# Differential attention: each query block split once and placed by transfers two heads ahead, norms over two heads at a time

## The chip, the cores and the metric

The program runs on one core of one Trainium2 chip. The metric is device time in microseconds (us) of one execution, the median over several executions. The core has a matrix engine (TensorE, PE in the rows, with its weight loads shown as PEld), three engines for elementwise work (VectorE or DVE, ScalarE or ACT, GpSimd or POOL), and a queue engine, SyncE or SP, that issues transfers. Each engine works through its own list of instructions in order and waits on semaphores of the others.

## The reference

Two layers of a hybrid block run over 512 latent tokens and a prefix of 256 context tokens, width 1024. What matters here is head group B, differential attention: 4 heads, each with two query/key halves of 64 columns (m = 0, 1) and one value of 128 columns. Behind it the output of a head is normed and joined with the other groups by an output projection:

```python
def diff_attn(q, k, v, lam):
    s = jnp.einsum("bqhmd,bkhmd->bhmqk", q, k) * (B_QK_DIM ** -0.5)
    p = jax.nn.softmax(s, axis=-1)
    a = p[:, :, 0] - lam * p[:, :, 1]
    return jnp.einsum("bhqk,bkhd->bqhd", a, v)
...
    yb = rms_norm(o, P["subln_g"]) * (1.0 - lam_init)
...
    return jnp.concatenate([ya, yb, yc], axis=-1) @ P["w_out"]
```

Latent queries see 512 latent and 256 context keys in one softmax; context queries see the 256 context keys, and only in the first layer are their outputs needed.

## The kernel before

Large products are made in a split form: a number is written as a high part that TensorE takes at its faster rate (fp32r) and the rest as a second fp32r number, so that a product is two or three matmuls. `sub_lo(o, a, hi)` (line 119) makes the rest, a subtraction on VectorE; a cast makes the high part. `act(...)` (line 110) is a ScalarE function, `flip` (line 122) a transpose on TensorE.

The attention stage of a layer (lines 845 to 1000) goes over a list of what the code numbers by `n`: a head and a block of 256 queries. In layer 0 these are 4 heads of context (2 key tiles of 128, so 256 keys) and then 8 of latent (4 heads, two blocks of 256 queries each, 6 key tiles, 768 keys); in layer 1 only the 8 of latent. The text calls each of them a head, context or latent. A head has two halves of 128 queries, `units (n, i)`. For a unit the loop calls `scores` and `combine`; two units later `transp` turns the weights around, three units later `attn_v` multiplies them with the values once for both halves, and five units later `subln` norms the head's output:

- `q_prep(n)`: TensorE transposes the queries into `pq`; ScalarE casts them once to `qn`; then the high part has to lie in both halves of the partitions, once for each m, and ScalarE and GpSimd copy it there, two 64x256 casts each (line 882). The rest goes to one of two tiles `qlz`, half of which was filled with zeros once per layer (lines 849 to 855), by two `sub_lo` of 64x256. Head 0 is cast straight from `pq` by four ScalarE casts (line 872).
- `scores(n, i)`: for each m two matmuls per stretch of keys (high, line 899, and rest, line 900), the row maximum on VectorE (`mx`, line 902) and the exponential with its sum on ScalarE (`e`).
- `combine(n, i)`: on VectorE `cc` (lines 915 and 916) and `e0 += cc*e1` (line 918); on GpSimd `dg`, a diagonal tile with epsilon times the squared sum (line 919): the weights are not divided by their sum, so the norm's epsilon is scaled instead.
- `transp(n, i)`: transposes into `pat`; the copies into `ath` are ScalarE's for the first four key tiles (line 935) and VectorE's for the last two (line 937).
- `attn_v(n)`: `po`, the copy `o`, its square `osq` (both ScalarE), and `osq + dg` on GpSimd (line 952).
- `subln(n)`: a product with ones (`pr`, line 959), logarithm and exponential (ScalarE), `o*gsub*osq` (VectorE, line 962), and the two parts `yBh` (ScalarE, line 964) and `yBl` (VectorE, line 119).

In the loop head n+1's queries are made when head n's first unit begins. Between these, TensorE takes parts of the output projection that don't need group B, `wo` in the rows, as filler; their weights are loaded through SP (`raw<-in_w_out_dram`), split into `whi` (ScalarE) and `wlo` (VectorE or GpSimd), and their sums added into `xT` (line 835). The order on each engine is decided when the program is built, by a list scheduler with priorities: the loop gives the emission order, `tc.high_priority(offset=SCP)` moves q_prep and scores ahead, and fillers go where the scheduler thinks that TensorE is free.

## Time and profile before

| | us |
|---|---|
| three runs | 1578.26, 1577.02, 1573.16 |
| their median | 1577.02 |
| the profiled execution | 1576.31 |
| its span, first to last instruction | 1574.5 |

The profile is of one execution; 1.8 us of its time lie around the span. Positions are us from the start of the span. The attention stage of layer 0 goes from about 237 to 345, that of layer 1 from about 1101 to 1186. Rows give, for a group of instructions, the count, the busy time, the mean duration of one, and the idle time of the engine just before with what ended it. A matmul's listed duration has a modelled tail that the next one overlaps, so a TensorE that shows as busy can be less than full.

### The profile page before, as it was taken

Reading aid. Unit: us, or ns where it says so; the run is one execution under the profiler, and the core shown is the slowest. Engines: PE = TensorE matmul, PEld = TensorE weight load, DVE = VectorE, ACT = ScalarE, POOL = GpSimd, SP = SyncE. Lnnn points to the kernel's source line nnn. Section 1 sums busy time; section 2 is a strip of 40 time slices with the busy share of each in tenths; the row PEclk is TensorE's granted clock in tenths of the full one; section 3 lists DMA queues with packets and bytes.
Section 4 is the critical chain, followed back from the end, with each engine's and each line's share of the span. In section 5 each row is a group of like instructions: output and inputs, shape, how many; then the busy total and the mean of one; then the engine's idle time right before and its main releaser. Section 6 shows DMA issues by size and latency. Waiting matters only on the chain.

```text
span 1574.5 us, 22904 instructions
## 1 busy us (share of the span) xinstructions
PE 1537.3 (98%) x8804; PEld 1305.1 (83%) x8804; DVE 1128.5 (72%) x1916; ACT 693.3 (44%) x1212; POOL 125.0 (8%) x144
## 2 busy tenths in 40 slices
PE   6999998999999999999999999999999999999999
PEld 4767776778788888888888887887778798998897
DVE  4489878969999982555555556796996974785673
ACT  5423578752532221123334234245774663463461
POOL 1102125310000000000000000000421200000000
PEclk9999999999999999999999999999999999999999
DMA  7651110015265885666877867653002353453432
GB/s 284 236 200 64 54 54 14 14 42 200 69 195 185 281 266 181 239 211 212 287 255 249 286 228 250 202 174 107 28 16 79 124 171 108 166 187 116 154 115 94
DMA packets 89486, 251.89 MB, mean 160 GB/s; under 512 B 12960, under 2 KB 15264, under 8 KB 89248
## 3 DMA queue, kind: packets, MB, share of 16 engines
q1 hardware_dynamic: 89376, 250.43, 47.6%
q8 instruction: 69, 1.13, 0.3%
q14 instruction: 41, 0.34, 0.1%
HBM read 211.59 MB, written 38.80 MB: 159 GB/s over the span
## 4 chain that ended last, share of the span: by engine, by line
PE 74%; DVE 3%; ACT 1%; issue 0%; POOL 0%; DVEq 0%; ACTq 0%; POOLq 0%
PE pp L359 9%; PE pp L358 9%; PE pp L360 9%; PE pd L358 7%; PE pd L360 7%; PE pd L359 7%; PE sv L358 4%; PE sv L359 4%; PE sv L360 4%; PE acc L528 2%; PE acc L536 2%; PE acc L529 2%; PE wo L358 2%; PE wo L359 2%; PE wo L360 2%; PE po L947 1%
## 5 line engine op out<-in xcount | busy, mean ns | idle before, releaser
L119 DVE TENSOR_TENSOR wlo<-raw,whi 128x1024 fp32r<-128x1024 f32 (+2 forms) x176 | 209.8, 1195 | 165.5 <-ACT whi L271 139.7
L271 ACT CAST whi<-raw 128x1024 fp32r<-128x1024 f32 (+1 forms) x137 | 139.5, 1021 | 402.3 <-PE pd L359 152.7
L359 PE MATMUL pp<-hlo,whi 128*128 128x256 f32 (+1 forms) x784 | 267.0, 342 | 1.5 <-DVE hlo L401 1.1
L358 PE MATMUL pp<-hhi,whi 128*128 128x256 f32 (+1 forms) x784 | 266.1, 341 | 1.3 <-ACT whi L271 1.0
L360 PE MATMUL pp<-hhi,wlo 128*128 128x256 f32 (+1 forms) x784 | 265.0, 339 | 0.0
L358 PE MATMUL pd<-gh,whi 128*128 128x512 f32 (+1 forms) x540 | 191.2, 354 | 0.0
L359 PE MATMUL pd<-gl,whi 128*128 128x512 f32 (+1 forms) x540 | 190.6, 353 | 0.0
L360 PE MATMUL pd<-gh,wlo 128*128 128x512 f32 (+1 forms) x540 | 190.6, 353 | 0.0
L359 PEld LDWEIGHTS pp<-hlo,whi 128*128 128x128 f32 x784 | 147.4, 188 | 22.8 <-DVE hlo L401 4.8
L358 PEld LDWEIGHTS pp<-hhi,whi 128*128 128x128 f32 x784 | 147.3, 188 | 22.0 <-ACT whi L271 2.5
L360 PEld LDWEIGHTS pp<-hhi,wlo 128*128 128x128 f32 x784 | 147.4, 188 | 18.2 <-DVE wlo L119 0.2
L360 PEld LDWEIGHTS pd<-gh,wlo 128*128 128x128 f32 x540 | 101.5, 188 | 15.6
L359 PEld LDWEIGHTS pd<-gl,whi 128*128 128x128 f32 x540 | 101.6, 188 | 15.2
L358 PEld LDWEIGHTS pd<-gh,whi 128*128 128x128 f32 x540 | 101.5, 188 | 15.1
L778 DVE SCALAR_TENSOR_TENSOR cacc<-cin,cw,cacc 128x783 f32<-128x783 f32 (+1 forms) x120 | 104.9, 925 | 3.4 <-ACT cacc L773 3.4
L243 DVE CUSTOM_DVE_ANT_0 mraw<-mraw,csil,bmod 128x1024 f32<-128x1024 f32 x64 | 81.6, 1278 | 5.9 <-DMA mraw<-in_w_modT_dram 5.7
L359 PE MATMUL sv<-hlo,whi 128*128 128x256 f32 x288 | 81.2, 282 | 0.0
L358 PE MATMUL sv<-hhi,whi 128*128 128x256 f32 x288 | 81.1, 282 | 0.0
L360 PE MATMUL sv<-hhi,wlo 128*128 128x256 f32 x288 | 81.1, 282 | 0.0
L1174 ACT CAST whi<-raw 128x1024 fp32r<-128x1024 f32 x54 | 56.5, 1050 | 51.2 <-PE sv L359 32.8
L528 PE MATMUL acc<-whi,hhi 128*128 128x512 f32 x192 | 78.6, 409 | 0.0
L529 PE MATMUL acc<-whi,hlo 128*128 128x512 f32 x192 | 76.5, 399 | 0.0
(279 smaller groups left out, 3335.2 us busy)
## 6 DMA issues: line engine op xcount, KB each, us to landing
raw<-in_w_gv_dram SPq DMA_DIRECT2D x78, 512.0 KB, 4.1
mraw<-in_w_modT_dram SPq DMA_DIRECT2D x64, 512.0 KB, 4.3
raw<-in_w_down_dram SPq DMA_DIRECT2D x37, 512.0 KB, 3.9
pgv<-in_w_gv_dram SPq DMA_DIRECT2D x28, 512.0 KB, 5.5
gv<-pgv SPq DMA_DIRECT2D x28, 512.0 KB, 4.7
raw<-gv SPq DMA_DIRECT2D x28, 512.0 KB, 3.8
wh<-in SPq DMA_DIRECT2D x24, 512.0 KB, 4.5
wl<-in SPq DMA_DIRECT2D x24, 512.0 KB, 4.6
```

The source lines that it names most:

```text
L119: return (eng or V).tensor_sub(o, a, hi.bitcast(F32))
L243: r = V.tensor_tensor_reduce(out=junk, in0=w, in1=csil[:, s], scale=1.0, scalar=bmod[:, l, i, f:f + 1], op0=ALU.mult, op1=ALU.add, accum_o ...
L271: S.copy(hi, raw)
L358: T.matmul(o, lhi, rhi, start=start, stop=False, skip_group_check=again)
L359: T.matmul(o, lhi, rlo, start=False, stop=False, skip_group_check=again)
L360: T.matmul(o, llo, rhi, start=False, stop=stop, skip_group_check=again)
L528: T.matmul(pt[t], hhi[hs], wh[:, a], start=k2 + a == 0, stop=False)
L529: T.matmul(pt[t], hlo[hs], wh[:, a], start=False, stop=False)
L536: T.matmul(pt[t], hhi[hs], wl[:, a], start=False, stop=k2 + 1 == KD // 2 and a == 1)
L778: V.scalar_tensor_tensor(out=cacc[:, c, :cn], in0=cin[:, c, j:j + cn], scalar=cw[:, l, c, j:j + 1], in1=cacc[:, c, :cn], op0=ALU.mult, op1 ...
L947: T.matmul(po, vt[:, kt, hs], at[:, c], start=c == 0, stop=c == nk - 1)
L1174: S.copy(hi, src)
```

## The change

The zero-filled tiles are gone. One tile `qq` holds for a head the high part and the rest, both laid out in both halves of the partitions. For head 0 it is made straight from `pq`, by four ScalarE casts and four `sub_lo` of 64x256. For every other head ScalarE makes one cast and VectorE one `sub_lo` of 128x256 into `qn`, and four transfers of 64 partitions x 2 x 256 numbers (128 KB), issued on SP, place them in `qq`. The queries of head n+2 instead of n+1 are made at head n's first unit. The norm (square, the epsilon addition, the product with ones, logarithm, exponential, scaling, the two parts) is done once for two heads on 128x512 instead of once per head on 128x256, and the epsilon addition is on VectorE instead of GpSimd. In the second half of a head the copy of the last two key tiles into `ath` is on ScalarE instead of VectorE.

```diff
--- before.py
+++ after.py
@@ -845,14 +845,6 @@
             ps = psum_pool(ph, f"ps2_{l}")
             gsub = sp.tile([P, 1], F32, name="gsub")
             V.tensor_scalar_mul(gsub, sublt[:, l:l + 1], 1.0 - lam0)
-
-            qlz = [sp.tile([P, 2, 256], F32R, name=f"qlz{x}") for x in range(2)]
-            zero = sp.tile([P, 256], F32, name="zero")
-            G.memset(zero, 0.0)
-            for x in qlz:
-                for m in range(2):
-                    ms = slice((1 - m) * QKD, (2 - m) * QKD)
-                    G.tensor_copy(x[ms, m], zero[ms])
             pairs = [(h, p) for p in range(2) for h in range(HEADS)]
             if not last:
                 pairs = [(h, 2) for h in range(HEADS)] + pairs
@@ -860,30 +852,29 @@
             st = {}
 
             def q_prep(n):
+
+
                 h, p = pairs[n]
-                qh = sp.tile([P, 2, 256], F32R, tag="qh", name="qh", bufs=QB)
-                ql = qlz[n % 2]
+                qq = sp.tile([P, 2, 2, 256], F32R, tag="qq", name="qq", bufs=QB)
                 pq = ps.tile([P, 256], F32, tag="w", name="pq", bufs=WB)
                 for i in range(2):
                     T.transpose(pq[:, i * P:(i + 1) * P], qt[2 * p + i][:, h * P:(h + 1) * P], ident)
                 if n == 0:
                     for m in range(2):
+                        src = pq[m * QKD:(m + 1) * QKD]
                         for a in range(2):
-                            S.copy(qh[a * QKD:(a + 1) * QKD, m], pq[m * QKD:(m + 1) * QKD])
+                            S.copy(qq[a * QKD:(a + 1) * QKD, 0, m], src)
+                        for a in range(2):
+                            sub_lo(qq[a * QKD:(a + 1) * QKD, 1, m], src, qq[m * QKD:(m + 1) * QKD, 0, m])
+                else:
+                    qn = sp.tile([P, 2, 256], F32R, tag="qn", name="qn", bufs=2)
+                    S.copy(qn[:, 0], pq)
+                    sub_lo(qn[:, 1], pq, qn[:, 0])
                     for m in range(2):
-                        ms = slice(m * QKD, (m + 1) * QKD)
-                        sub_lo(ql[ms, m], pq[ms], qh[ms, m])
-                else:
-                    qn = sp.tile([P, 256], F32R, tag="qn", name="qn", bufs=2)
-                    S.copy(qn, pq)
-                    for m in range(2):
-                        src = qn[m * QKD:(m + 1) * QKD]
                         for a in range(2):
-                            (G.tensor_copy if a else S.copy)(qh[a * QKD:(a + 1) * QKD, m], src)
-                    for m in range(2):
-                        ms = slice(m * QKD, (m + 1) * QKD)
-                        sub_lo(ql[ms, m], pq[ms], qn[ms])
-                st["q", n] = (qh, ql)
+                            nc.sync.dma_start(out=qq[a * QKD:(a + 1) * QKD, :, m].bitcast(F32),
+                                              in_=qn[m * QKD:(m + 1) * QKD].bitcast(F32))
+                st["q", n] = (qq[:, 0], qq[:, 1])
 
             def scores(n, i):
                 h, p = pairs[n]
@@ -909,9 +900,9 @@
                 nk = 6 if pairs[n][1] < 2 else 2
                 e, sm = st[n, i]
                 cc = sp.tile([P, 1], F32, tag="cc", name="cc", bufs=4)
-                if i == 0:
-                    st["dg", n] = sp.tile([P, 2, P], F32, tag="dg", name="dg", bufs=3)
-                dg = st["dg", n][:, i]
+                if i == 0 and n % 2 == 0:
+                    st["dg", n // 2] = sp.tile([P, 2, 256], F32, tag="dg", name="dg", bufs=3)
+                dg = st["dg", n // 2][:, n % 2, i * P:(i + 1) * P]
                 V.reciprocal(out=cc, in_=sm[:, 1:2])
                 V.scalar_tensor_tensor(out=cc, in0=cc, scalar=nlam, in1=sm[:, 0:1], op0=ALU.mult, op1=ALU.mult)
                 e0, e1 = e[0][:, :nk * P], e[1][:, :nk * P]
@@ -931,7 +922,7 @@
                     for c in range(cn_):
                         flip(pat[:, c], e[:, (c0 + c) * P:(c0 + c + 1) * P])
                     osl = (slice(None), slice(c0, c0 + cn_), slice(i * P, (i + 1) * P))
-                    if c0 == 0:
+                    if c0 == 0 or i == 1:
                         S.copy(at[osl], pat[:, :cn_])
                     else:
                         V.tensor_copy(at[osl], pat[:, :cn_])
@@ -945,24 +936,25 @@
                 for c in range(nk):
                     kt = k0 // P + c
                     T.matmul(po, vt[:, kt, hs], at[:, c], start=c == 0, stop=c == nk - 1)
-                o = sp.tile([P, 256], F32, tag="o", name="o", bufs=2)
-                sq = sp.tile([P, 256], F32, tag="osq", name="osq", bufs=2)
-                S.copy(o, po)
+                if n % 2 == 0:
+                    st["sub", n // 2] = sp.tile([P, 2, 256], F32, tag="o", name="o", bufs=2)
+                S.copy(st["sub", n // 2][:, n % 2], po)
+
+            def subln(x):
+
+                h, p = pairs[2 * x]
+                o = st["sub", x]
+                sq = sp.tile([P, 2, 256], F32, tag="osq", name="osq", bufs=2)
                 S.activation(sq, o, AF.Square)
-                G.tensor_add(sq, sq, st["dg", n].rearrange("p a q -> p (a q)"))
-                st["sub", n] = (o, sq)
-
-            def subln(n):
-                h, p = pairs[n]
-                o, sq = st["sub", n]
-                pr = ps.tile([P, 256], F32, tag="w", name="pr", bufs=WB)
-                T.matmul(pr, ones, sq, start=True, stop=True)
+                V.tensor_add(sq, sq, st["dg", x])
+                pr = ps.tile([P, 2, 256], F32, tag="w", name="pr", bufs=WB)
+                T.matmul(pr.rearrange("p y q -> p (y q)"), ones, sq.rearrange("p y q -> p (y q)"), start=True, stop=True)
                 act(sq, pr, AF.Ln, scale=1.0 / P)
                 act(sq, sq, AF.Exp, scale=-0.5)
                 V.scalar_tensor_tensor(out=o, in0=o, scalar=gsub, in1=sq, op0=ALU.mult, op1=ALU.mult)
-                ts = slice(p * 256, p * 256 + 256)
-                S.copy(yBh[:, h, ts], o)
-                sub_lo(yBl[:, h, ts], o, yBh[:, h, ts])
+                osl = (slice(None), slice(h, h + 2), slice(p * 256, p * 256 + 256))
+                S.copy(yBh[osl], o)
+                sub_lo(yBl[osl], o, yBh[osl])
 
             first = [(g, i) for g in whole for i in range(2)]
             if l == 0:
@@ -970,13 +962,14 @@
                 g, i = first.pop(0)
                 wout(0, (0,), w0, [g], ps, "f", FB, (i,))
             q_prep(0)
+            q_prep(1)
             nu = len(units)
             for u in range(nu + 8):
                 if u < nu:
                     n, i = units[u]
-                    if i == 0 and n + 1 < len(pairs):
+                    if i == 0 and n + 2 < len(pairs):
                         with tc.high_priority(offset=SCP):
-                            q_prep(n + 1)
+                            q_prep(n + 2)
                     with tc.high_priority(offset=SCP):
                         scores(n, i)
                     combine(n, i)
@@ -987,8 +980,8 @@
                 if 0 <= v < nu and units[v][1] == 1:
                     attn_v(units[v][0])
                 v = u - LAG[2]
-                if 0 <= v < nu and units[v][1] == 1:
-                    subln(units[v][0])
+                if 0 <= v < nu and units[v][1] == 1 and units[v][0] % 2 == 1:
+                    subln(units[v][0] // 2)
 
             for mp2 in range(NFILL[l]):
                 if mp2 == 0 and l == 0:
```

The order of instructions moves with it. The first place is VectorE at the beginning of layer 0's attention stage, with head 0 (`pq_2096` before, `pq_2088` after) and head 1 (`pq_2106`, `pq_2100`). Before:

```order
L835 SCALAR_TENSOR_TENSOR xT_61<-wo_2081,modv_67,xT_61 128x256 [waits PE_49]
L119 TENSOR_TENSOR qlz0_2067<-pq_2096,qh_2095 64x256 [waits PE_49,Activation_49]
L119 TENSOR_TENSOR qlz0_2067<-pq_2096,qh_2095 64x256
L902 TENSOR_REDUCE mx_2121<-pss_2118 128x1 [waits PE_49]
L902 TENSOR_REDUCE mx_2128<-pss_2125 128x1 [waits PE_49]
L119 TENSOR_TENSOR qlz1_2068<-pq_2106,qn_2109 64x256 [waits Activation_49]
L119 TENSOR_TENSOR qlz1_2068<-pq_2106,qn_2109 64x256
L915 RECIPROCAL cc_2132<-sm_2117 128x1 [waits Activation_49]
L902 TENSOR_REDUCE mx_2142<-pss_2139 128x1 [waits PE_49]
```

After, where `qn_2103` is head 1's tile and `qn_2114` head 2's:

```order
L835 SCALAR_TENSOR_TENSOR xT_61<-wo_2073,modv_67,xT_61 128x256 [waits PE_49]
L119 TENSOR_TENSOR qq_2087<-pq_2088,qq_2087 64x256 [waits PE_49,Activation_49]
L119 TENSOR_TENSOR qq_2087<-pq_2088,qq_2087 64x256
L119 TENSOR_TENSOR qn_2103<-pq_2100,qn_2103 128x256 [waits Activation_49]
L893 TENSOR_REDUCE mx_2125<-pss_2122 128x1 [waits PE_49]
L119 TENSOR_TENSOR qq_2087<-pq_2088,qq_2087 64x256 [waits Activation_49]
L119 TENSOR_TENSOR qq_2087<-pq_2088,qq_2087 64x256
L119 TENSOR_TENSOR qn_2114<-pq_2111,qn_2114 128x256
L893 TENSOR_REDUCE mx_2132<-pss_2129 128x1 [waits PE_49]
```

Head 0 now has four subtractions, and one subtraction each for heads 1 and 2 stands between them and the first maxima. The second place is SP at the same time, from a load of output weights on; `raw_3516` is the load that was issued at 238.51. Before:

```order
L263 DMA raw_3398<-in_w_out_dram 128x1024 [waits DMAHW5_49,Pool_49]
L263 DMA raw_3516<-in_w_out_dram 128x1024 [waits DMAHW6_49,Pool_49]
L263 DMA raw_3522<-in_w_out_dram 128x1024 [waits DMAHW7_49,DVE_49]
L263 DMA raw_3644<-in_w_out_dram 128x1024 [waits DMAHW0_49,DVE_49]
L240 DMA mraw_3336<-in_w_modT_dram 128x1024 [waits PE_49]
```

After, where `raw_3427` is that load, `qq_2099` head 1's tile, `qq_2110` head 2's and `qq_2162` head 3's:

```order
L263 DMA raw_3309<-in_w_out_dram 128x1024 [waits DMAHW5_49,Pool_49]
L263 DMA raw_3427<-in_w_out_dram 128x1024 [waits DMAHW6_49,Pool_49]
L875 DMA qq_2099<-qn_2103 64x2x256 [waits DVE_49]
L875 DMA qq_2099<-qn_2103 64x2x256 x3
L875 DMA qq_2110<-qn_2114 64x2x256 [waits DVE_49,Activation_49]
L875 DMA qq_2110<-qn_2114 64x2x256 [waits DMAHW7_49]
L875 DMA qq_2110<-qn_2114 64x2x256 [waits DMAHW0_49]
L875 DMA qq_2110<-qn_2114 64x2x256 [waits DMAHW1_49]
L875 DMA qq_2162<-qn_2166 64x2x256 [waits DMAHW2_49,DVE_49,PE_49]
L875 DMA qq_2162<-qn_2166 64x2x256 [waits DMAHW3_49]
L875 DMA qq_2162<-qn_2166 64x2x256 [waits DMAHW4_49]
L875 DMA qq_2162<-qn_2166 64x2x256 [waits DMAHW5_49]
```

The transfers of each head follow the weight loads on the one queue, and wait for VectorE (the rest is made), from head 3 on for TensorE too (the tile is free). The third place is TensorE at the end of layer 0's stage, from the last product with the values (`po`) on. Before, with the last two `pr`:

```order
L947 MATMUL po_3183<-ath_3143,vt_1268 128x256 [waits DVE_49]
L947 MATMUL po_3183<-ath_3143,vt_1268 128x256
L959 MATMUL pr_3195<-osq_3162,ones_64 128x256 [waits PE_49,Pool_49]
L358 MATMUL wo_3299<-yACh_86,whi_3253 128x512 [waits DVE_49]
L359 MATMUL wo_3299<-yACl_87,whi_3253 128x512
L360 MATMUL wo_3299<-yACh_86,wlo_3254 128x512
L358 MATMUL wo_3299<-yACh_86,whi_3253 128x512
L959 MATMUL pr_3202<-osq_3191,ones_64 128x256 [waits PE_49,Pool_49]
L359 MATMUL wo_3299<-yACl_87,whi_3253 128x512
L360 MATMUL wo_3299<-yACh_86,wlo_3254 128x512
```

After, with the one last `pr`, for two heads:

```order
L938 MATMUL po_3102<-ath_3062,vt_1268 128x256 [waits Activation_49]
L938 MATMUL po_3102<-ath_3062,vt_1268 128x256 x3
L938 MATMUL po_3102<-ath_3062,vt_1268 128x256 [waits Activation_49]
L938 MATMUL po_3102<-ath_3062,vt_1268 128x256
L951 MATMUL pr_3113<-osq_3110,ones_64 128x512 [waits DVE_49,PE_49]
L358 MATMUL wo_3315<-yACh_86,whi_3305 128x256
L359 MATMUL wo_3315<-yACl_87,whi_3305 128x256
L360 MATMUL wo_3315<-yACh_86,wlo_3306 128x256
L358 MATMUL wo_3315<-yACh_86,whi_3305 128x256
```

Before, four filler matmuls stand between the next to last and the last `pr`; now the last `pr` follows the last `po` directly.

## Rows read from the trace of the kernel before

**Rows 1.** The page, part 1: busy us, share of the span, instructions.

```profile
PE 1537.3 (98%) x8804; PEld 1305.1 (83%) x8804; DVE 1128.5 (72%) x1916; ACT 693.3 (44%) x1212; POOL 125.0 (8%) x144
```

**Rows 2.** Stretches: length, then busy us of PE, PEld, DVE, ACT, POOL, granted clock.

```profile
237.00:254.00 17.00, 13.34 (x70) 11.12 (x69) 12.92 (x40) 13.36 (x46) 9.33 (x19) 0.80 0.10 31
254.00:340.00 86.00, 80.19 (x436) 65.58 (x436) 77.33 (x149) 66.72 (x165) 28.32 (x44) 1.00 0.02 7
1102.00:1181.00 79.00, 74.83 (x399) 60.72 (x398) 71.86 (x132) 60.72 (x140) 27.86 (x43) 1.00 0.07 22
```

**Rows 3.** Groups by shape, layer 0, 237 to 345.

```profile
L902 DVE TENSOR_REDUCE mx<-pss 128x1 f32<-128x768 f32 x32 | 30.1, 949 | 1.5 <-PE pss L900 1.3
L119 DVE TENSOR_TENSOR qlz<-pq,qn 64x256 fp32r<-64x256 f32 x22 | 9.2, 418 | 0.4
L882 ACT CAST qh<-qn 64x256 fp32r<-64x256 f32 x22 | 8.9, 404 | 0.3
L937 DVE COPY ath<-pat 128x256 f32<-128x256 f32 x16 | 6.4, 412 | 1.7 <-PE pat L122 1.6
L935 ACT COPY ath<-pat 128x256 f32<-128x256 f32 x8 | 3.0, 372 | 0.8 <-PE pat L122 0.8
L962 DVE SCALAR_TENSOR_TENSOR o<-o,gsub,osq 128x256 f32<-128x256 f32 x12 | 7.1, 593 | 2.9 <-ACT osq L110 2.8
L119 DVE TENSOR_TENSOR yBl<-o,yBh 128x256 fp32r<-128x256 f32 x11 | 4.6, 418 | 1.7 <-ACT yBh L964 1.6
L952 POOL TENSOR_TENSOR osq<-osq,dg 128x256 f32<-128x256 f32 x12 | 10.6, 886 | 23.9 <-ACT osq L951 23.9
```

**Rows 4.** Groups at 128x512, the whole execution.

```profile
L119 DVE TENSOR_TENSOR a22l<-a,a22h 128x512 fp32r<-128x512 f32 x18 | 12.3, 685 | 0.6 <-ACT a22h L1193 0.6
L394 DVE SCALAR_TENSOR_TENSOR nt<-xT,amod,nrs 128x512 f32<-128x512 f32 x24 | 17.5, 746 | 5.1 <-ACT nrs L110 5.1
L380 ACT ACTIVATE nsq<-xT 128x512 f32<-128x512 f32 x21 | 13.1, 628 | 13.4 <-DVE xT L835 7.5 <-DVE xT L1327 4.8 <-DVE nss L381 0.9
```

**Rows 5.** What TensorE waited for, 236 to 345: us in total, times, longest.

```profile
PE pss L899 <- ACT e L110: 5.7, 8, 1.1
PE pss L899 <- POOL qh L882: 1.6, 2, 1.1
```

**Rows 6.** The same, layer 1, 1101 to 1186.

```profile
PE pat L122 <- DVE e L918: 1.9, 3, 0.8
```

**Rows 7.** Timeline of the end of layer 0's stage: start, us, engine, instruction.

```profile
340.13 0.37 ACT L950 COPY o<-po 128x256 f32<-128x256 f32 x1 [1.38 <-PE po L947]
341.70 0.48 DVE L962 SCALAR_TENSOR_TENSOR o<-o,gsub,osq 128x256 f32<-128x256 f32 x1 [2.50 <-ACT osq L110]
341.86 0.70 PE L959 MATMUL pr<-osq,ones 128*128 128x256 f32 x2 [0.42 <-POOL osq L952]
342.87 0.40 PE L358 MATMUL wo<-yACh,whi 128*128 128x512 f32 x1
343.11 0.39 PE L359 MATMUL wo<-yACl,whi 128*128 128x512 f32 x1
```

**Rows 8.** Timeline of the beginning of layer 0's stage.

```profile
238.51 0.33 SPq L263 DMA_DIRECT2D raw<-in_w_out_dram  x1
239.20 0.88 DVE L119 TENSOR_TENSOR qlz<-pq,qh 64x256 fp32r<-64x256 f32 x2 [1.28 <-ACT qh L872]
243.34 0.36 PE L899 MATMUL pss<-kk,qh 128*128 128x256 f32 x1 [0.89 <-ACT e L110]
247.76 0.55 PE L899 MATMUL pss<-kk,qh 128*128 128x256 f32 x1 [1.08 <-POOL qh L882]
```

**Rows 9.** DMA issues, whole execution: count, KB each, median us to landing.

```profile
in<-ahi SPq DMA_DIRECT2D x40, 256.0 KB, 4.5
out_dram<-xT SPq DMA_DIRECT2D x4, 128.0 KB, 1.8
```

**Rows 10.** Two short stretches of layer 0, same columns.

```profile
246.00:252.00 6.00, 4.92 (x20) 4.19 (x19) 4.00 (x14) 4.36 (x15) 1.71 (x4) 0.50 0.00 0
265.00:275.00 10.00, 7.60 (x45) 5.97 (x43) 9.62 (x20) 8.38 (x21) 5.10 (x8) 1.00 0.00 0
```

## The prediction, made before the changed kernel ran

> **What bounds the kernel now.** I read the page's engine shares first: TensorE is busy 98% of the span [rows 1], so outside the stages that this change touches nothing is to be had. Then I cut the two attention stages into stretches [rows 2]. The reader is to see three things there. The stretch 237 to 254, the context heads of layer 0, keeps no engine full: of 17.0 us TensorE is busy 13.3, VectorE 12.9, ScalarE 13.4, and the granted clock is 0.80. The latent part of layer 0 (86.0 us) has VectorE at 77.3 and TensorE at 80.2, layer 1 (79.0 us) VectorE at 71.9 and TensorE at 74.8. And these TensorE numbers flatter it: a filler matmul of 512 columns is listed with 0.40 us, but the next starts 0.24 us later [rows 7], so short gaps between matmuls count as busy. VectorE's numbers have no such tail; it is busy 91% in layer 1, with small idle pieces that its own in-order list makes.
>
> Next, the waits. In layer 0 TensorE waited 5.7 us for the exponentials (ScalarE, which itself waits for VectorE's maxima) and 1.6 us for GpSimd's copies of the queries [rows 5]; in layer 1 the largest wait is on VectorE's `e`, 1.9 us [rows 6]. So the chain of a latent head is maxima, exponential, `e`, transposes; VectorE is the engine with least to spare, and a microsecond taken from its list should come back nearly whole where TensorE has room.
>
> **VectorE, per latent head.** The split: two subtractions of 418 ns become one on 128 partitions; the 128x256 `yBl` costs 418 too, so one is saved, 0.42. The `ath` copy of the second half goes to ScalarE, 0.41. The scaling `o` at 128x256 has a mean of 593, stretched by a few long ones; an undisturbed one has 0.48 [rows 7], which I take; at 128x512 the like form costs 746, half of it 373, so 0.11 is saved. `yBl`: 418 against 685/2, 0.08. The epsilon addition comes in: 685/2, 0.34. Together 0.42 + 0.41 + 0.11 + 0.08 - 0.34 = 0.68 us saved per latent head [rows 3, 4]. A context head has no `ath` copy on VectorE: 0.27.
>
> Head 0 of each layer goes the other way: four subtractions of 64x256 where two stood. It misses the 0.42 and adds 0.84, so 1.26 per layer.
>
> Layer 0: 8 x 0.68 + 4 x 0.27 - 1.26 = 5.3 us of VectorE. Layer 1: 8 x 0.68 - 1.26 = 4.2 us.
>
> **ScalarE and GpSimd.** ScalarE loses two casts of 404 ns per head and gains a copy of 372, and its four norm instructions run at double width [rows 3]. It gets lighter, by 0.44 per latent head before the norms are counted; it isn't the bound, so I count nothing. GpSimd loses 886 per head (the addition) and two casts; it never was the bound, but TensorE's 1.6 us of waits for it in the context part go [rows 5]: -1.6.
>
> **The end of the stage.** Before, the last `pr` waited 0.42 us, with filler ahead of it [rows 7]. Now no filler stands between the last `po` and the last `pr`, and ahead of that come copy 0.37 [rows 7], square 0.63 and addition 0.685 at double width [rows 4]: 1.68 us, net +1.3 in layer 0. In layer 1 ten filler matmuls at 0.24 cover it: 0.
>
> **The transfers.** Four per head, 128 KB each. An issue takes 0.33 us on SP [rows 8]. Their flight isn't in this trace: no transfer here goes from on-chip memory to on-chip memory. Bounds from the nearest rows: 1.8 us (128 KB, out) and 4.5 us (256 KB, out, on a busy queue) [rows 9]. From first issue to last landing T = 4 x 0.33 + 1.8 = 3.1, or 1.3 + 4.5 = 5.8. I take 3.9, nearer the low end, since the size is the same and the queue is nearly empty here; all this is an estimate. Who waits: head 1 of layer 0. Its subtraction can end at about 239.2 + 0.88 + 0.42 = 240.5, and its scores began at 243.34 before [rows 8], so it is late by T - 2.8: +1.0 at T = 3.9, between 0.3 and 3.0. Later context heads last 247.76 - 243.34 = 4.4 us [rows 8], two of them 8.8; a head's queries need transposes, a cast, a subtraction and their turn, which I put at 2.5, so T up to 6.3 is hidden. Latent heads last 79/8 = 9.9 us [rows 2], two of them 20: hidden with room. On SP the weight load issued at 238.51 is just ahead of head 1's transfers; behind them stands a later weight load whose split isn't needed for several heads.
>
> The Trainium skill ("DMA: Bandwidth & Descriptors", Anatomy of one DMA) fits one transfer as about 2.0 us plus its bytes over 436e3 per us, and says under Bandwidth to batch to 1 MiB or more. That speaks against four pieces of 128 KB: 2.3 us each by the fit, and 9.2 for a head if they went one behind another, which would make this change slower by the formula of the second rival. The trace has 1.8 us for such a size; no run here yet shows whether four overlap.
>
> **The clock.** From 246 to 252 the granted clock is 0.50, the lower level (1.2 of 2.4 GHz), and TensorE's 4.9 busy us there would be about half at the upper [rows 10]; before it, TensorE was often idle. The new order gives the context heads more filler, so it may stay up. I count -1.0 of a possible 2.5, because other engines share that stretch.
>
> **Sum.** Layer 0: -5.3 - 1.6 + 1.3 + 1.0 - 1.0 = -5.6. Layer 1: the 4.2 of VectorE meets a TensorE that shows 4.2 us idle in 79 [rows 2], and not each saved piece lies on the chain; I take two thirds, -2.8. Together -8.4 against the profiled 1576.3: 1567.9. That execution is 0.7 below the median of the three (1577.0), well within their spread of 5, so I forecast 1568.
>
> **The rivals.** (1) The saved work is not on the chain. The epsilon addition now sits in VectorE's list and waits for ScalarE's square; behind it are the maxima and `e` of the running heads, and all matmuls wait for those. If each of the 10 pairs holds VectorE up by 0.6 us, 6 of the 8.4 us are gone: 1574, no change. For it: ScalarE showed waits in turn on VectorE. Against: the addition is placed well behind the square, which is on an engine that is idle for 18 of 79 us [rows 2].
>
> (2) The other side: the transfers come late. With the terms above but the +1.0, the total is -9.4 + (T - 2.8) + 4 x (T - 6.3), the last from T = 6.3 on. At T = 7.2 (four times 1.8 in turn) that is -1.4; no gain from about 7.5, and at 9 (four in turn at 2.25) it is +7.6, so 1584. Against it: transfers of this kernel overlap elsewhere.
>
> (3) The filler is spent on the context heads and is missing later, in latent heads, where TensorE then idles enough to be granted the lower level: at half clock the 74.8/8 = 9.4 us that a head's matmuls show [rows 2] would need up to twice that in a period of 9.9, up to +9; with half of that, 4.5, for four heads it is +18, so 1586. Against it: from 265 to 275 TensorE shows 7.6 busy of 10 at clock 1.00 [rows 10].
>
> (4) More than forecast: fewer waits multiply, since ScalarE too gets lighter and GpSimd leaves VectorE's memory accesses alone, as the mean 593 of `o` [rows 3] against 0.48 for one alone [rows 7] hints. With 0.1 us off each of 32 `e` operations (-3.2), the whole 4.2 in layer 1 and the full 2.5 of the clock: 1568 - 3.2 - 1.4 - 1.5 = 1562, and down to 1556 with the 5.7 of [rows 5] gone as well. The Trainium skill ("GPSIMD Engine Reference", Specifications) has GpSimd share its memory interfaces with VectorE, with contention for operations with two inputs in memory; by that, `e`, `o` and `yBl` get faster. No row here separates it.
>
> (5) The change does not do what it says: the scheduler's new order keeps the old waits under other names, and only GpSimd's 1.6 us and the end's 1.3 remain, nearly nothing together: 1576, counted with (1).
>
> **How the numbers follow.** Forecast, 1563 to 1572: 0.50. More (4), 1554 to 1563: 0.14. Swallowed (1, 5), 1572 to 1580: 0.20. Late transfers (2), 1580 to 1600: 0.11. Clock (3), 1580 to 1600: 0.05. A difference under 0.3% (4.7 us) can't be told from no change. Faster: 0.50 + 0.14 = 0.64; same 0.20; slower 0.16. The range leaves out 0.16 above and a little of (4): 1559 to 1580. The likeliest case has 1563 to 1572 for itself.
>
> **What would show it.** VectorE's busy time lower by about 5 and 4 us in the two stages; the two-head addition at about 0.69; no wait of TensorE on GpSimd in scores; scores of head 1 at about 244.5, and no scores after that waiting for a transfer; a wait of 1.7 us at the last `pr` of layer 0. Wrong would be: scores waiting for transfers beyond head 1, a clock under 1.00 in latent heads, VectorE idle before the addition, or layer 1 as long as before with TensorE at its floor.

## The result, and the profile after

| | before | changed |
|---|---|---|
| median, us | 1575.32 (6 runs) | 1566.17 (1564.31 to 1567.57, 6 runs) |
| ratio of the two | | 0.9941, 95% interval 0.9926 to 0.9955 |
| profiled span, us | 1574.5 | 1565.5 |

9.2 us less; 8.4 were forecast, to 1568. The page, part 1, of the changed kernel, beside [rows 1]:

```profile
PE 1532.0 (98%) x8784; PEld 1301.7 (83%) x8784; DVE 1118.6 (71%) x1876; ACT 679.5 (43%) x1152; POOL 89.3 (6%) x78
```

VectorE lost 9.9 us, ScalarE 13.8, GpSimd 35.7. Stretches of the two stages, as in [rows 2] (length, then busy us of PE, PEld, DVE, ACT, POOL, granted clock, share of the transfer engines, GB/s):

```profile
237.00:254.00 17.00, 15.46 (x94) 12.91 (x92) 14.17 (x42) 11.07 (x41) 4.82 (x7) 1.00 0.63 154
254.00:338.00 84.00, 77.80 (x420) 62.83 (x419) 71.98 (x127) 62.97 (x139) 12.17 (x18) 0.99 0.27 70
1095.00:1174.00 79.00, 75.35 (x401) 60.65 (x399) 69.00 (x118) 58.04 (x124) 14.82 (x17) 1.00 0.29 74
```

The context part now has TensorE at 15.5 of 17 us and the clock at 1.00, where it was 13.3 and 0.80. The groups that answer to [rows 3 to 4], layer 0, 236 to 345:

```profile
L893 DVE TENSOR_REDUCE mx<-pss 128x1 f32<-128x768 f32 x32 | 30.4, 952 | 2.6 <-PE pss L891 2.3
L909 DVE SCALAR_TENSOR_TENSOR e<-e,cc 128x768 f32<-128x768 f32 x16 | 16.3, 1021 | 0.2
L119 DVE TENSOR_TENSOR qn<-pq,qn 128x256 fp32r<-128x256 f32 x11 | 4.6, 414 | 0.1
L954 DVE SCALAR_TENSOR_TENSOR o<-o,gsub,osq 128x512 f32<-128x512 f32 x6 | 4.5, 746 | 5.1 <-ACT osq L110 5.1
L119 DVE TENSOR_TENSOR yBl<-o,yBh 128x512 fp32r<-128x512 f32 x6 | 4.1, 689 | 2.1 <-ACT yBh L956 1.9
L949 DVE TENSOR_TENSOR osq<-osq,dg 128x512 f32<-128x512 f32 x6 | 4.1, 684 | 1.5 <-ACT osq L948 1.4
L928 DVE COPY ath<-pat 128x256 f32<-128x256 f32 x8 | 3.3, 415 | 0.1
```

Each unit price of the sum is there as worked out: 414, 746, 689, 684 ns. What TensorE waited for, 230 to 345, as in [rows 5]:

```profile
PE pss L890 <- ACT e L110: 3.3, 5, 1.2
PE pr L951 <- DVE osq L949: 2.0, 1, 2.0
PE pat L122 <- DVE e L909: 1.5, 3, 0.7
```

No wait on GpSimd is left; the wait for exponentials went from 5.7 to 3.3. The 2.0 is the last `pr`. The end of the stage on the timeline, as in [rows 7]:

```profile
334.26 0.37 ACT L941 COPY o<-po 128x256 f32<-128x256 f32 x1 [0.98 <-PE po L938]
334.66 0.63 ACT L948 ACTIVATE osq<-o 128x512 f32<-128x512 f32 x1
335.39 0.69 DVE L949 TENSOR_TENSOR osq<-osq,dg 128x512 f32<-128x512 f32 x1 [1.39 <-ACT osq L948]
336.23 1.33 PE L951 MATMUL pr<-osq,ones 128*128 128x512 f32 x2 [2.01 <-DVE osq L949]
```

Copy, square, addition, as forecast, 2.0 instead of 1.7. The transfers, as in [rows 8] and [rows 9]: first issue on SP, first scores of head 1, and the landing (count, KB, median us):

```profile
239.80 0.66 SPq L875 DMA_DIRECT2D qq<-qn  x1
```

```profile
243.77 0.28 PE L890 MATMUL pss<-kk,qq 128*128 128x256 f32 x1
```

```profile
qq<-qn SPq DMA_DIRECT2D x44, 128.0 KB, 2.4
```

A landing takes 2.4 us from the start of its issue, not the 1.8 of [rows 9]. The fit of the Trainium skill ("DMA: Bandwidth & Descriptors", Anatomy of one DMA), which the page gives for transfers issued by GpSimd, has 2.3 for this size; the 2.4 measured for issues on SP is close to it. An issue takes 0.6 us, not 0.33.

To compare kernels I cut each stage by starts on the timeline: a stage goes from the first `pss` matmul to the first `wo` that reads `yBh`; inside it, the context part goes to the first scores of the first latent head, and "7 heads" from there to the first scores of the last latent head; the end is what is left. The last column is the sum of VectorE's (ScalarE's) durations in the 7 heads of layer 0, per head; neighbours overlap, so it counts some time twice and can exceed the period of a head. How full an engine is shows in its busy time, which counts overlapped time once (7 heads before, changed, and placed by copies; columns as in [rows 2]):

```profile
257.48:323.65 66.17, 60.60 (x336) 49.78 (x335) 62.23 (x118) 53.47 (x130) 23.85 (x36) 1.00 0.03 9
256.16:316.51 60.35, 58.08 (x323) 47.36 (x322) 56.11 (x100) 47.07 (x104) 8.77 (x14) 1.00 0.28 66
256.39:320.47 64.08, 61.44 (x331) 48.94 (x330) 59.09 (x103) 55.33 (x120) 20.26 (x27) 1.00 0.05 17
```

From before to changed, VectorE's busy time falls by 6.1 us, 0.87 per head where 0.68 was forecast, and the 7 heads get 5.8 us shorter. That fits the forecast's mechanism but does not single it out, since ScalarE's falls by 6.4.

| us | layer 0: stage | context | 7 heads | end | layer 1: stage | 7 heads | end | VectorE's (ScalarE's) list |
|---|---|---|---|---|---|---|---|---|
| before | 108.4 | 19.0 | 66.2 | 23.2 | 86.9 | 62.0 | 24.9 | 9.8 (8.9) |
| changed | 101.4 | 17.7 | 60.3 | 23.4 | 85.1 | 58.7 | 26.4 | 8.8 (7.9) |
| copy back on VectorE | 99.8 | 17.7 | 60.0 | 22.1 | 84.1 | 59.1 | 25.0 | 9.1 (7.6) |
| epsilon on GpSimd | 104.4 | 19.2 | 61.9 | 23.2 | 84.8 | 58.6 | 26.2 | 8.8 (7.9) |
| epsilon left out | 98.2 | 17.7 | 59.9 | 20.6 | 84.4 | 58.7 | 25.8 | 8.5 (7.9) |
| one subtraction more | 103.8 | 18.5 | 62.6 | 22.7 | 86.7 | 65.3 | 21.4 | 9.2 (7.8) |
| two casts more | 102.9 | 19.3 | 60.9 | 22.6 | 82.7 | 59.4 | 23.3 | 8.8 (8.6) |
| placed by copies | 105.1 | 19.1 | 64.1 | 21.9 | 89.0 | 60.3 | 28.7 | 9.3 (9.3) |
| one head ahead | 102.8 | 19.1 | 61.4 | 22.2 | 83.6 | 58.9 | 24.7 | 8.7 (7.9) |

Of the 9.0 us between the two spans, layer 0's stage gave 6.9 and layer 1's 1.8. Each line is one execution, and each edit also moves filler between loop and end, so a stage's total says more than its parts. How far is seen with one subtraction more: in layer 1's 7 heads 58 filler matmuls instead of 42, and an end 5 us shorter.

### The profile page after: what moved, and what is told of

It reads as the page before. It is cut to its first block, busy times and chain, and to the rows that moved or that the text cites. A ratio compares the mean times of both kernels' runs of the same rounds, so it can differ in the third digit from the quotient of the medians.

```text
span 1565.5 us, 22804 instructions
## 1 busy us (share of the span) xinstructions
PE 1532.0 (98%) x8784; PEld 1301.7 (83%) x8784; DVE 1118.6 (71%) x1876; ACT 679.5 (43%) x1152; POOL 89.3 (6%) x78
## 4 chain that ended last, share of the span: by engine, by line
PE 91%; DVE 5%; ACT 2%; issue 1%; DMA 1%; SPq 0%; DVEq 0%; ACTq 0%
PE pp L359 9%; PE pp L358 9%; PE pp L360 9%; PE pd L360 7%; PE pd L359 7%; PE pd L358 7%; PE acc L528 5%; PE acc L536 5%; PE acc L529 5%; PE sv L358 4%; PE sv L359 4%; PE sv L360 4%; PE po L938 2%; PE wo L358 2%; PE wo L359 2%; PE wo L360 2%
## 5 line engine op out<-in xcount | busy, mean ns | idle before, releaser
L359 PEld LDWEIGHTS pp<-hlo,whi 128*128 128x128 f32 x784 | 147.3, 188 | 22.7 <-DVE hlo L401 4.8
L359 PEld LDWEIGHTS pd<-gl,whi 128*128 128x128 f32 x540 | 101.4, 188 | 15.2
```

What stands on the lines that cost most here:

```text
L359: T.matmul(o, lhi, rlo, start=False, stop=False, skip_group_check=again)
```

## The experiments

The ratios are to the kernel before, measured beside it; the changed kernel has 0.9941. Differences in us between two changed kernels are of medians from different runs; the kernel before had medians from 1575.3 to 1576.5 in them, so about 1 us of such a difference means nothing.

**The copy back on VectorE.**

```diff
-                    if c0 == 0 or i == 1:
+                    if c0 == 0:
```

> The changed kernel with one part undone: in the second half of a head the copy of the last two key tiles is VectorE's again (16 copies of 0.41 us, 6.6 us back on VectorE; ScalarE loses 16 of 0.37). If VectorE's list is what bounds the latent heads, more than half of the 6.6 us comes back as time: 4 to 6 us slower than the changed kernel, so about 4 us faster than before. If ScalarE was the bound, it is no slower than the changed kernel (9 us faster than before) or better. If TensorE bounds, no difference either.

1563.76 us, 0.9924 (0.9912 to 0.9937): 2.4 us faster than the changed kernel where 4 to 6 slower was expected of a VectorE bound. The loops kept their length with VectorE's list 0.3 us longer per head; the ends are 1.3 and 1.4 us shorter. Moving this copy gained nothing and probably cost, though the intervals of the two ratios overlap. Of all kernels that compute everything this is the fastest.

**The epsilon addition back on GpSimd.**

```diff
-                V.tensor_add(sq, sq, st["dg", x])
+                G.tensor_add(sq, sq, st["dg", x])
```

> The changed kernel with the epsilon addition on GpSimd (10 additions of 128x512). VectorE loses 10 x 0.69 = 6.9 us. If VectorE's busy time alone counts: 3 to 5 us faster than the changed kernel, so 12 to 14 us faster than before. If the addition on GpSimd costs twice (it takes about 1.5 us at the ends of the stages, where nothing covers it, and slows VectorE's operations with two inputs), the gain is gone: within 2 us of the changed kernel.

1568.38 us, 0.9948 (0.9934 to 0.9962): no gain. Groups of layer 0 in this kernel:

```profile
L909 DVE SCALAR_TENSOR_TENSOR e<-e,cc 128x768 f32<-128x768 f32 x16 | 17.1, 1068 | 0.2
L949 POOL TENSOR_TENSOR osq<-osq,dg 128x512 f32<-128x512 f32 x6 | 7.9, 1309 | 17.4 <-issue 9.3 <-ACT osq L948 4.5 <-DVE e L909 3.1
L907 DVE SCALAR_TENSOR_TENSOR cc<-cc,nlam,sm 128x1 f32<-128x1 f32 x24 | 6.8, 281 | 0.4
```

The addition takes 1309 instead of 684 ns, and the means of VectorE's own `e` and `cc` rise, from 1021 to 1068 and from 215 to 281, so VectorE's list stays at 8.8 although the addition is gone from it. The means hide how: shortest, median and longest of the 24 `e` and `cc` of layer 0, context heads included, are

```profile
L909 DVE SCALAR_TENSOR_TENSOR e<-e,cc x24: 470/1007/1916, 243.7 to 330.4; 128x768 f32<-128x768 f32 x16, 128x256 f32<-128x256 f32 x8
L907 DVE SCALAR_TENSOR_TENSOR cc<-cc,nlam,sm x24: 203/219/1289, 243.5 to 330.2; 128x1 f32<-128x1 f32 x24
```

The medians are those of the changed kernel (1009 and 216). A few operations that meet an addition are held up: the `cc` of 1289 ns starts with the addition at 272.52 and ends with it, the `e` of 1916 starts 0.2 us after the one at 308.58. The Trainium skill ("GPSIMD Engine Reference", Specifications) has the two engines share their memory interfaces, with contention for VectorE operations with two inputs in memory; the trace agrees for these. This profile also has the half clock in the context part (242.8 to 246.2), so not all of its 104.4 us is the addition's.

**The norms alone, on the kernel before** (`attn_v`, `subln` and the call of `subln` as in the change, the rest as before).

```diff
-                G.tensor_add(sq, sq, st["dg", n].rearrange("p a q -> p (a q)"))
+                V.tensor_add(sq, sq, st["dg", x])
...
-                if 0 <= v < nu and units[v][1] == 1:
+                if 0 <= v < nu and units[v][1] == 1 and units[v][0] % 2 == 1:
```

> The kernel before with one part of the change alone: norms for two heads at once and the epsilon addition on VectorE. VectorE per head: minus 0.11 minus 0.08 plus 0.34, so 0.15 more, about 3 us over 20 heads; ScalarE about 0.3 less per head. If VectorE bounds: 0 to 3 us slower than before. If ScalarE, or GpSimd's late additions, bound: 3 to 5 us faster than before.

1573.91 us, 0.9989 (0.9981 to 0.9998): 2 us, or none.

**The queries one head ahead.**

```diff
-            q_prep(1)
...
-                    if i == 0 and n + 2 < len(pairs):
+                    if i == 0 and n + 1 < len(pairs):
...
-                            q_prep(n + 2)
+                            q_prep(n + 1)
```

> The changed kernel with the queries made one head ahead instead of two. Four issues of 0.6 us and a landing of 2.4 us, as the changed kernel shows, are 4.8 us; with 2.5 us for making the queries, 7.3 us against 4.4 us of a context head and 9.9 of a latent one. If the distance of two heads matters where I said, each of the four context heads is late by up to 2.9 us: 5 to 11 us slower than the changed kernel, all of it in layer 0 before 260, layer 1 as long as in the changed kernel. If the transfers are hidden anyway: within 1.5 us of the changed kernel.

1567.89 us, 0.9947 (0.9934 to 0.9959): the same as the changed kernel within the intervals. The context part lasts 19.1 instead of 17.7 us, but it starts 1.5 us earlier (236.98 against 238.49) and ends at the same time, 256.1. So no gain of the second head of distance is shown, in layer 0 or in layer 1.

**The queries' part alone, on the kernel before** (`q_prep` and its calls as in the change, norms per head, no copy moved; the edit, cut here to its last lines, is shown against the changed kernel).

```diff
...
-                if 0 <= v < nu and units[v][1] == 1 and units[v][0] % 2 == 1:
-                    subln(units[v][0] // 2)
+                if 0 <= v < nu and units[v][1] == 1:
+                    subln(units[v][0])
```

> The kernel before with the queries' part of the change alone: split once, placed by transfers, two heads ahead; norms per head with GpSimd's addition, and the copies into the attention tile as before. VectorE loses 0.42 us per head (7.5 us) and gains 2.5 us at heads 0; ScalarE loses 0.81 us per head. If the runs so far add up (norms alone about 2 us faster than before, the moved copy about 2.5 us slower), this is where the time comes from: 9 to 11 us faster than before. If the parts only work together: 3 to 6 us faster.

1574.29 us, 0.9987 (0.9979 to 0.9996), although layer 0's stage is down to 102.3. Layer 1's is 91.1, 4.2 longer than before. Its end in stretches, and TensorE's longest wait there:

```profile
1096.00:1168.00 72.00, 68.25 (x369) 55.27 (x368) 66.49 (x122) 52.85 (x120) 20.39 (x23) 1.00 0.28 69
1168.00:1172.00 4.00, 4.00 (x13) 3.16 (x12) 2.33 (x3) 1.31 (x2) 0.00 (x0) 0.58 0.27 108
1172.00:1181.00 9.00, 7.28 (x35) 5.61 (x33) 3.93 (x7) 4.32 (x12) 2.14 (x2) 1.00 0.20 67
1181.00:1190.00 9.00, 8.80 (x32) 7.08 (x33) 3.37 (x6) 3.83 (x6) 0.00 (x0) 0.81 0.24 79
```

```profile
PE pr L950 <- POOL osq L943: 1.7, 1, 1.7
```

TensorE waits twice 0.9 us for ScalarE's copies into `ath` (at 1165.8 and 1167.2), and later 1.7 us for GpSimd's last addition; each time the half clock follows, from 1167.9 to 1171.3 and from 1181.6 to 1185.0. The profiled execution is the slowest of the twelve (1576.46; the others go down to 1571.23), so not every one of them need have both.

**The same with the addition on VectorE.**

```diff
-                G.tensor_add(sq, sq, st["dg", n].rearrange("p a q -> p (a q)"))
+                V.tensor_add(sq, sq, st["dg", n].rearrange("p a q -> p (a q)"))
```

> The kernel with the queries' part of the change alone, norms per head, but with the epsilon addition on VectorE (128x256, 0.42 us, one per head) instead of GpSimd. If GpSimd's late additions are what cost layer 1's end there (a wait of 1.7 us, and the lower clock behind it): layer 1's stage falls by 4 to 6 us from 91.1, while layer 0 gains nothing or loses about 2. If the end is long for another reason (filler used up, weights late): layer 1 stays within 1.5 us of 91.

1566.98 us, 0.9938 (0.9925 to 0.9950): the whole gain of the change, without norms in pairs and without the moved copy. Layer 1's stage is 85.4 us, 5.7 of the 8.0 us between the two spans; layer 0's stays at 102.3. The wait for the last addition and both stretches at half clock are gone in layer 1; why the first of the two went, behind waits for ScalarE, is not shown. The same stretches:

```profile
1168.00:1172.00 4.00, 3.58 (x18) 3.12 (x18) 3.90 (x9) 2.91 (x6) 0.00 (x0) 1.00 0.16 65
1172.00:1181.00 9.00, 8.74 (x41) 6.89 (x40) 4.71 (x11) 5.69 (x15) 0.00 (x0) 1.00 0.17 61
1181.00:1190.00 9.00, 9.00 (x41) 7.33 (x40) 3.12 (x4) 2.79 (x4) 0.00 (x0) 1.00 0.17 58
```

**Placed by copies instead of transfers.**

```diff
-                            nc.sync.dma_start(out=qq[a * QKD:(a + 1) * QKD, :, m].bitcast(F32),
-                                              in_=qn[m * QKD:(m + 1) * QKD].bitcast(F32))
+                            (G.tensor_copy if a else S.copy)(qq[a * QKD:(a + 1) * QKD, :, m], qn[m * QKD:(m + 1) * QKD])
```

> The changed kernel with the four transfers of a head replaced by copies of 64x512, two on ScalarE and two on GpSimd (as the kernel before did for the high part alone). VectorE's list stays as in the changed kernel; ScalarE gets two copies of about 0.6 us per head back, 22 us in all. If VectorE's saved subtraction is the gain: within 2 us of the changed kernel. If ScalarE's saved casts are the gain: 6 us or more slower than the changed kernel, so 3 us or less faster than before.

1573.92 us, 0.9988 (0.9980 to 0.9997). So the split once hardly pays without the transfers, or with these copies in their place. Why is open. ScalarE's list adds up to 9.3 us per latent head of layer 0, against a period of 64.1/7 = 9.2, but without the overlap it is busy for 55.3 of 64.1 us (the last line of busy times in the section on the result), so it isn't full. The copies also give GpSimd two per head (628 ns), and VectorE's `cc` goes from 215 to 246 and its `yBl` from 689 to 754. The half clock follows a 2.0 us wait at the last `pr` in both layers instead of one. No run has the copies on ScalarE alone.

**One more subtraction on VectorE**, and **two more casts on ScalarE**, both into a tile that nothing reads.

```diff
+                    qd = sp.tile([P, 256], F32R, tag="qd", name="qd", bufs=2)
+                    sub_lo(qd, pq, qn[:, 0])
```

> The changed kernel with one more subtraction of 128x256 per head on VectorE, into a tile that nothing reads: 18 x 0.42 = 7.5 us of VectorE, at the place of the subtraction that the change took away. If VectorE bounds the stages: 4 to 7 us slower than the changed kernel. If ScalarE does: under 2 us.

```diff
+                    qd = sp.tile([P, 256], F32R, tag="qd", name="qd", bufs=2)
+                    for m in range(2):
+                        S.copy(qd[m * QKD:(m + 1) * QKD], qn[m * QKD:(m + 1) * QKD, 0])
```

> The changed kernel with two more casts of 64x256 per head on ScalarE, into a tile that nothing reads: 18 x 0.81 = 14.5 us of ScalarE, at the place of the casts that the change took away. If ScalarE bounds the stages: 7 to 14 us slower than the changed kernel. If VectorE does: under 3 us. Both bound in part: the two added loads each cost a half of theirs, 3 to 4 and 6 to 7 us.

The subtraction: 1570.38 us, 0.9969 (0.9957 to 0.9981), 4.2 us for 7.5 of VectorE; in the 7 heads of layer 0 it is 2.3 for the 2.5 of six subtractions. The casts: 1566.63 us, 0.9943 (0.9931 to 0.9955), 0.5 us for 14.5 of ScalarE.

**The epsilon addition left out** (the line `V.tensor_add(sq, sq, st["dg", x])` removed).

> The changed kernel without the epsilon addition (the norm's epsilon is left out of the result): 10 operations of 0.68 us off VectorE, and off the way from the last square to the last product with ones. If a latent head lasts as long as VectorE's list: about 0.3 us less per head from one latent head's scores to the next, 4 us over the loops, and 0.7 at each end, so 4 to 5 us faster than the changed kernel. If VectorE is full only because it waits for the others in its list, the loops keep their length and only the ends gain: 1 us or less.

1563.52 us, 0.9914 (0.9901 to 0.9928), 2.7 us. The 7 heads last 59.9 and 58.7 us, as with it (60.3 and 58.7), with 0.3 us less in VectorE's list; layer 0's end is 2.8 us shorter, layer 1's 0.6. In layer 0 the 2.0 us wait at the last `pr` and the half clock behind it are gone too. The second theory of the expectation holds for the loops, and the ends gain more than it said.

**More filler, on the kernel with the copy back.**

```diff
-NFILL = (2, 3)
+NFILL = (3, 3)
```

> The changed kernel with the copy back on VectorE (the best so far, 12 us faster than before) and a third group of output columns as TensorE filler in layer 0's attention stage instead of two. TensorE is idle for some 2 us at the last product with ones and some more between the latent heads. If this idle time is what is left to gain: 1 to 4 us faster than with the copy back alone. If the filler's weight splits (two casts of 1.05 us on ScalarE, two subtractions of 1.2 us on VectorE) load VectorE in the loop: no gain, or up to 2 us slower.

1567.25 us, 0.9942 (0.9929 to 0.9954): 3.5 us slower than without. The last wait for `pr` fell from 2.0 to 1.0 and no half clock follows it, but the 7 heads take 61.9 instead of 60.0.

**Eight transfers per head.**

```diff
-                            nc.sync.dma_start(out=qq[a * QKD:(a + 1) * QKD, :, m].bitcast(F32),
-                                              in_=qn[m * QKD:(m + 1) * QKD].bitcast(F32))
+                            for b in range(2):
+                                nc.sync.dma_start(out=qq[a * QKD:(a + 1) * QKD, b, m].bitcast(F32),
+                                                  in_=qn[m * QKD:(m + 1) * QKD, b].bitcast(F32))
```

> The changed kernel with eight transfers per head of 64 KB instead of four of 128 KB. An issue takes 0.6 us and a landing 2.3, so the time from first issue to last landing goes from 4.1 to 6.5 us. By the formula of the prediction's second rival head 1 of layer 0 is 2.4 us later and the next four heads 0.2 each: 3 us slower than the changed kernel. If the distance of two heads covers all but head 1 and the later ones catch up: 1 to 2 us slower. If issues of one queue hold each other up: 5 us slower or more.

1576.84 us, 0.9996 (0.9986 to 1.0007): by the median the whole gain is gone. The eleven runs lie between 1570.66 and 1579.23, and the profiled one is the slowest. In the context part each head's first issue follows the one before by 5.1 to 5.2 us (239.2, 244.3, 249.5, 254.6), eight times the 0.6 of an issue, and the part lasts 19.8 us: there SP's issuing sets the pace. The scores of heads 1 to 4 start 2.0 to 3.2 us before the last of their transfers has landed. Layer 0's stage is 4.0 us longer. Layer 1's is 6.1 longer, and not by lateness: its transfers are first issued 8 us or more ahead of their scores. Its end, after the same 2.0 us wait at `pr`, is granted the lower clock:

```profile
1180.00:1184.00 4.00, 2.04 (x10) 1.45 (x8) 1.82 (x3) 1.62 (x3) 0.00 (x0) 1.00 0.00 0
1184.00:1192.00 8.00, 7.27 (x17) 4.85 (x18) 1.45 (x2) 3.13 (x4) 0.00 (x0) 0.57 0.00 0
```

By my estimate about half of the 6.1 is that (7.3 busy us at 0.57); the rest is probably another distribution of filler that the scheduler chose (58 records in the loop, as with one subtraction more), which I have not tested apart.

## Why the prediction was right, step by step

**The total and its place.** 9.2 against 8.4. The step "Layer 0: -5.6" measured 6.9 in the profile, and layer 1's "-2.8" 1.8, inside what one execution and a moved filler can shift.

**The split.** Right in its sign and nearly in its size: VectorE saves one subtraction per head, and putting one back costs 4.2 of 7.5 us. But it needs the transfers: placed by copies, the gain of the whole change falls from 9.2 to about 2 us. The step "ScalarE gets lighter; it isn't the bound, so I count nothing" held where it was tested alone: 0.8 us per head more (two casts) cost nothing that can be told. Whether the two copies of 0.6 on ScalarE or the two on GpSimd cost the 7.7 us is not separated.

**The copy, 0.41 per latent head.** This step failed. It was the second largest term, 6.6 of the sum's VectorE time, and undoing it does not cost anything. Nor does VectorE's load set the length of the loops from here on: the 7 heads of layer 0 last 59.9 to 60.8 us for a busy VectorE of 53.9 (epsilon left out), 56.1 (the change), 56.7 (queries' part, epsilon on VectorE), 57.0 (copy back) and 58.2 us (queries' part alone), and 60.9 to 61.9 us for 55.5 to 57.6 in four others. One subtraction more does lengthen them, to 62.6 with VectorE busy for 57.3, so it costs by where it stands, or by what the scheduler did with it, and not by the load alone; which is not tested. What sets the loops I can't name: in the changed kernel's 7 heads TensorE waits 1.0 us for exponentials and 1.0 for `e`, VectorE 2.3 for scores and 1.0 for exponentials. TensorE is listed as busy for 58.1 of 60.3 us, where it was 60.6 of 66.2, so it is the nearest candidate, but with its modelled tails that isn't shown.

**The epsilon addition, charged with +0.34 per head.** The price was right as a duration (684 ns per pair), wrong as a cost. It was counted as 0.34 for each of 20 heads, 6.9 us of VectorE; leaving it out gains 2.7. On GpSimd it is as dear or dearer: it delays the ends and holds up some of VectorE's operations. This is the term that I had on the wrong side: with the queries' part, moving the addition alone is worth 7 us (1574.29 to 1566.98), mostly in layer 1's end. So two errors of about the same size, the copy counted as a gain (6.6) and the addition as a loss (6.9), nearly cancelled: that the total came out so close is in part luck.

**Norms in pairs, 0.19 per head.** Not separable: without pairs and without the moved copy the kernel has 0.9938, the changed one 0.9941; with pairs and without the moved copy 0.9924, whose interval overlaps.

**Two heads ahead and the transfers' T.** T, from head 1's first issue to its last landing, was forecast as 3.9 and is 4.5 (239.80 to 244.26). Both of its parts were too small, 0.33 for an issue and 1.8 for a landing against 0.6 and 2.4; their sum was 3.1, and 3.9 was picked above it. Head 1's scores start at 243.77, before the last landing, as those for m = 0 need only the first two transfers; they are 0.4 us later than in [rows 8], where +1.0 was forecast. Later heads aren't late: their last transfers land 0.8 us or more ahead of their scores. Rival 2 did not come. For eight transfers its formula gives +3; the context part is 2.1 us longer and layer 0's stage 4.0, which is near it. Most of the rest of the 10.7 us is in layer 1, where no transfer is late, and the formula has no term for that.

**The end and the clock.** The wait at the last `pr` is there (2.0 against 0.42 before). The half clock of [rows 10] is gone from the context part in every profile with the new queries' part except the one with the epsilon addition back on GpSimd (242.8 to 246.2), and present (244.0 to 250.8) with the norms alone. In the changed kernel's profile a shorter one, 337.0 to 340.4, follows the new wait. The sum has the wait's +1.3 but nothing for that clock.

**Rivals 1 and 3** did not come: the 7 heads run at clock 1.00, and VectorE waited 1.4 us, once, for the square. **Rival 4**'s mechanism, VectorE's operations freed from GpSimd, is small on average: `e` went from 1036 to 1021.

## What to carry to other kernels

Cost a moved operation by where its result is waited for, not only by the list that it leaves: on the path at a stage's end, an addition on the slow engine cost more than the same addition did in VectorE's list. A list whose durations add up to the period isn't a full engine: look at the busy time without overlap, and test both directions, since here neither taking VectorE time away nor giving some back moved the loop, and only an operation added at another place did. Placement between partitions by transfers held nobody up here but head 1 while the issuing queue's time per step (four times 0.6 us) was under the period of the step (4.4 us), and set the pace when it was over it (eight times).

## What the runs showed of the hardware that was not expected

An issue of a 64-partition transfer inside on-chip memory keeps SP for 0.6 us (median 0.61), about twice the 0.33 of a 512 KB load, and halving its size leaves that as it was (0.59). Half of the full clock follows most long waits at a stage's end: of the eleven waits of 2.0 us or more at a last `pr` in these profiles, nine have a stretch of it begin within 1.4 us of their end, and two (one subtraction more, layer 1; two casts more) have none. The matmuls in such a stretch (0.63 instead of 0.40 us listed) make the wait longer than it looks. One VectorE operation can take up to six times as long beside a GpSimd addition (`cc`, 1289 against 216 ns), while most of its kind keep their time.
